# Splitting 128-column fp32 products into two 64-column products on the two halves of PSUM

## The chip, the cores and the metric

The kernel runs on one core of one Trainium2 chip. The metric is device time in microseconds for one execution of the whole program. Of the kernel before, three runs were timed: 2756.0, 2758.8 and 2760.12 us, with a median of 2758.8 us.

## The reference

The program is a two-layer decoder trunk on 256 tokens and 2048 channels, all in fp32. Layer 0 mixes tokens with a gated DeltaNet (32 value heads, 16 key heads), layer 1 with HGRN2 (16 heads); each is followed by a SwiGLU feed-forward layer. Cut to what matters here:

```python
def gated_delta_rule_chunked(q, k, v, beta, g):      # GDN, chunks of 64 tokens
    A = strict_lower(kb @ k.T * decay)
    T = triangular_solve(eye + A, eye)               # per head and chunk
    u, w = T @ (v * b), T @ (kb * exp(G))
    for chunk:
        v_new = u - w @ S
        o = q_dec @ S + (q @ k.T * decay) @ v_new
        S = S * g_last + k_dec.T @ v_new

def hgrn2_chunked(q, k, v, logf):
    for chunk:
        o = q_dec @ S + scores @ v
        S = S * f_last + k_dec.T @ v

h = h + gdn_mixer(rmsnorm(h)); h = h + swiglu(rmsnorm(h))
h = h + hgrn2_mixer(rmsnorm(h)); h = h + swiglu(rmsnorm(h))
out = rmsnorm(h)
```

## The kernel before, in words

Nearly all arithmetic is the dense projections. Their weights stream from HBM in pieces of 128 x 1024 fp32 values (512 KB, here called halves), issued by SP into the tiles `raw`, of which there are four. ACT rounds each half into `wh` (type fp32r), DVE takes the remainder into `wl`, and TensorE adds three fp32r products (high x high, high x low, low x high) into the PSUM tiles `main`. One half feeds twelve products with 512 moving columns. These are the main products.

Between them lie the batches of the recurrences, which use plain fp32 operands and write the PSUM tiles `aux`. A plain fp32 product stands in the profile as two records (two weight loads and two matmuls), a main product as one. For each of the eight groups of four GDN heads these batches follow one another:

- In `gdn_qk` (line 1039), twice a group: `k` against `k` and `q` (`aux<-kqv`, 512 and 256 moving columns), and behind them two products of the squares `sq` with a single column of ones (`aux<-ones,sq`).
- In `gdn_inverse` (line 1129): `aux<-inv,nmat` and `aux<-u,pp`, first in blocks of 32 columns and then of 64. The 64-column blocks write the lower and the upper 64 partitions of PSUM in turn.
- In `gdn_o` (line 1302): `aux<-r,u`, `aux<-w,nmat`, again `aux<-r,u` (four products of 128 stationary and 128 moving columns each), and twelve in `aux<-w,dec`.

For each of the four groups of four HGRN heads, `hgrn_scores` (line 1487) has one batch of four products with 128 stationary and 128 moving columns (`aux<-qp,kp 128*128`), then three batches with 64 stationary columns and 32 or 64 moving ones (`aux<-qp,kp 128*64`, `aux<-q,k`), whose outputs go to the two PSUM halves in turn; `hgrn_o` (line 1624) has twelve products in one batch (`aux<-v,sc`, `aux<-v,cross`).

The order of all instructions is made when the program is built. Calls are recorded (class `Recorder`), and `plan` (line 310) plays them through on one clock for each engine, with a price for every operation from `price` (line 262), then issues them in the order it found, all from line 490. For fp32 products the price depends on the number of stationary columns, whatever moves: 0.075 us up to 64 columns, at least 0.224 us above that. Each change between main and recurrence products is priced at 0.06 us. `batches` (line 289) lets a batch start only when all that its products read is ready. On the chip every engine then runs its list strictly in order.

Two paths go through DRAM. `gdn_inverse` gathers a triangular matrix by four SP loads (`wide<-n_dram`, line 1135), which stand in SP's queue among the loads of weight halves; `conv_turned` (line 1004) and `through_dram` (line 769) transpose keys and queries by DMAs from the POOL queue into `kq_blocks`, which ACT copies to `pre`.

The function below prices the products; the functions after it hold those that the change touches.

```python
m = op.args[1].shape[1]
op.cost = 0.05 if m <= 32 else 0.075 if m <= 64 else max(FP32_PRODUCT, n * 1.69e-3)
```

Of the kernel before, what the change touches and what calls it, by code (L numbers as in the profile page):

```python
# [17 lines left out]
P = 128  # L18
T = 256
# [486 lines left out]
class Trunk:  # L506
# [282 lines left out]
    def keep_x(self):  # L789

        self.resident = self.nc.pool("resident", 1, phase=True)
        for cg in range(2):
            self.x[cg] = self.tile(self.resident, [P, 2, 512], f"resident{cg}")
            self.nc.gpsimd.dma_start(self.x[cg], self.x_cols(self.x_home, cg))

    def load_x(self, cg):
        if self.resident:
            return
        self.x[cg] = self.tile(self.xpool, [P, 2, 512], "x", ordered=True)
        self.nc.gpsimd.dma_start(self.x[cg], self.x_cols(self.x_at, cg))  # L800
# [238 lines left out]
    def gdn_qk(self, hg, pre, st):  # L1039
        nc = self.nc  # L1040
        t = lambda shape, tag, **kw: self.tile(self.pool, shape, tag, **kw)
        kq = t([P, 4, T], "kqv")
        self.conv_silu(pre, [16 + 2 * hg, 2 * hg, 17 + 2 * hg, 2 * hg + 1], kq)


        g_row = t([P, 1024], "g_row")
        nc.gpsimd.dma_start(
            g_row,
            self.g_rows[4 * hg : 4 * hg + 4, :].rearrange("h t -> (h t)").unsqueeze(0).broadcast_to([P, 1024]),
        )  # L1050
        rows = g_row.rearrange("p (h c s) -> p h c s", h=4, s=CH)
        dec = t([P, 4, 384], "dec", bufs=2)
        for tt in range(2):
            part = dec[:, :, tt * T : tt * T + T - tt * P]
            for c in range(4 - 2 * tt):
                for h in range(4):
                    at = 4 * tt + c
                    nc.scalar.activation(
                        part[:, h, c * CH : (c + 1) * CH], rows[:, h, 2 * tt + c, :], AF.Relu,
                        bias=self.shift[:, 4 * hg + h, at : at + 1], scale=-1.0,  # L1060
                    )
        nc.scalar.activation(dec, dec, AF.Exp, scale=-1.0)
        for tt in range(2):
            own = dec[:, :, tt * T : tt * T + P]
            nc.gpsimd.affine_select(
                out=own, in_=own, pattern=[[0, 4], [1, P]], compare_op=ALU.is_ge, fill=0.0,
                base=0, channel_multiplier=-1,
            )


        ss, pw, rec = (t([P, 2, 4], n, bufs=2) for n in ("ssqk", "pwqk", "recqk"))
        nmat = t([P, 4, 384], "nmat", bufs=2)
        for kh in range(2):
            k = kq[:, 2 * kh, :]
            both = kq[:, 2 * kh : 2 * kh + 2, :]
            ps0, ps1 = self.aux(), self.aux()
            nc.together(ps0, ps1, nmat)
            nc.after(dec)
            nc.tensor.matmul(
                ps0, k[:, 0:P], both.rearrange("p a t -> p (a t)"), start=True, stop=True  # L1080
            )
            nc.after(dec)
            nc.tensor.matmul(
                ps1[:, 0:T].rearrange("p (a t) -> p a t", a=2), k[:, P:T], both[:, :, P:T],
                start=True, stop=True,
            )
            sq = t([P, T], "sq", bufs=2)
            nc.scalar.activation(sq, both[:, 1, :], AF.Square)
            for tt in range(2):
                nc.tensor.matmul(  # L1090
                    ps1[:, T + tt : T + tt + 1], sq[:, tt * P : (tt + 1) * P], self.ones[:, 0:1],
                    start=True, stop=True,
                )
            for tt, ps in enumerate((ps0, ps1)):
                nc.vector.scalar_tensor_tensor(
                    out=self.vjunk[:, 0:P], in0=ps[:, 0:P], scalar=1.0, in1=self.ident,
                    op0=ALU.mult, op1=ALU.mult, accum_out=ss[:, kh, 2 * tt : 2 * tt + 1],
                )
            nc.vector.tensor_copy(ss[:, kh, 1:4:2], ps1[:, T : T + 2])
            nc.vector.tensor_scalar(  # L1100
                out=ss[:, kh, :], in0=ss[:, kh, :], scalar1=1e-6, scalar2=None, op0=ALU.add
            )
            nc.gpsimd.tensor_tensor(out=pw[:, kh, :], in0=ss[:, kh, :], in1=self.expo, op=ALU.pow)
            nc.vector.reciprocal(out=rec[:, kh, :], in_=ss[:, kh, :])
            heads = slice(2 * kh, 2 * kh + 2)
            for ps, tt, w in ((ps0, 0, T), (ps1, 1, P)):
                d = dec[:, heads, tt * T : tt * T + w]
                for at, o in ((0, nmat[:, heads, tt * T : tt * T + w]), (w, d)):
                    nc.vector.scalar_tensor_tensor(
                        out=o, in0=ps[:, at : at + w].unsqueeze(1).broadcast_to([P, 2, w]),  # L1110
                        scalar=rec[:, kh, 2 * tt : 2 * tt + 1], in1=d, op0=ALU.mult, op1=ALU.mult,
                    )
        pw = pw.rearrange("p k (t c) -> p k t c", c=2)
        st["inv_k"], st["q_scale"] = pw[:, :, :, 0], pw[:, :, :, 1].rearrange("p k t -> p t k")
        st["n"], st["scores"] = nmat, dec


        n_dram = self.tile(self.dram, [32, 32, 32], "n_dram")
        u_dram = self.tile(self.dram, [32, 32, 32], "u_dram")
        for q in range(4):  # L1120
            b = slice(32 * q, 32 * q + 32)
            for tt in range(2):
                nc.gpsimd.dma_start(
                    n_dram[8 * q + 4 * tt : 8 * q + 4 * tt + 4].rearrange("a j i -> j a i"),
                    nmat[b, :, 256 * tt + 32 * q : 256 * tt + 32 * q + 32],
                )
        st["n_dram"], st["u_dram"] = n_dram, u_dram
# [174 lines left out]
    def gdn_o(self, hg, st):  # L1302
        nc = self.nc
        n, sc, u, r = st["n"], st["scores"], st["u"], st["r"]

        def heads(ps, lhs, rhs, start=True, stop=True):
            for h in range(4):
                nc.tensor.matmul(ps[:, h * P : (h + 1) * P], lhs(h), rhs(h), start=start, stop=stop)

        def evac(ps):  # L1310
            w = self.tile(self.pool, [P, 512], "w", bufs=2)
            nc.scalar.activation(w, ps, AF.Copy)
            return lambda h: w[:, h * P : (h + 1) * P]

        ps = self.aux()
        heads(ps, lambda h: u[:, h, :], lambda h: r[:, 0, h, :])
        w1 = evac(ps)
        ps = self.aux()
        heads(ps, lambda h: n[:, h, P:T], w1)
        r1 = r[:, 1, :, :].rearrange("p h d -> p (h d)")  # L1320
        nc.vector.tensor_tensor(out=r1, in0=r1, in1=ps, op=ALU.subtract)
        ps = self.aux()
        heads(ps, lambda h: u[:, 4 + h, :], lambda h: r[:, 1, h, :])
        w2 = evac(ps)
        o = [self.aux(), self.aux()]
        nc.together(*o)
        nc.after(w2(0))
        heads(o[0], lambda h: sc[:, h, 0:P], w1)
        for h in range(4):
            s = o[1][:, h * P : (h + 1) * P]  # L1330
            nc.after(w2(0))
            nc.tensor.matmul(s, sc[:, h, P:T], w1(h), start=True, stop=False)
            nc.tensor.matmul(s, sc[:, h, T:384], w2(h), start=False, stop=True)
        scale = self.tile(self.pool, [P, 8], "oscale")
        nc.vector.tensor_single_scalar(
            out=scale.rearrange("p (t k e) -> p t k e", t=2, e=2),
            in_=st["q_scale"].unsqueeze(3).broadcast_to([P, 2, 2, 2]),
            scalar=float(P) ** -0.5, op=ALU.mult,
        )
        st["ot"] = self.head_out(  # L1340
            o, st["zs"], scale, self.gdn_hn, r.rearrange("p t h d -> p (t h d)")
        )
# [144 lines left out]
    def hgrn_scores(self, g, rows, st):  # L1487
        nc = self.nc
# [27 lines left out]
        tt(qp, q[:, :, P:T], e[:, :, P:T], ALU.mult)  # L1516
        ps = self.aux()
        for h in range(4):
            nc.tensor.matmul(
                ps[:, h * P : (h + 1) * P], kp[:, h, 0:P], qp[:, h, :], start=True, stop=True  # L1520
            )
        cross = t([P, 512], "cross", bufs=2)
        nc.scalar.activation(cross, ps, AF.Copy)
        st["cross"] = cross
# [60 lines left out]
        for n in range(0, len(LEVELS), 2):  # L1585
            ps = self.aux()
# [37 lines left out]
    def hgrn_o(self, g, st):  # L1624
# [4 lines left out]
        for tok in range(2):  # L1629
            for h in range(4):  # L1630
                s = slice(h * P, (h + 1) * P)
                if tok:
                    nc.after(sc)
                    nc.tensor.matmul(o[1][:, s], cross[:, s], v[:, 0, s], start=True, stop=False)
                nc.tensor.matmul(
                    o[tok][:, s], sc[:, 2 * h + tok, :], v[:, tok, s], start=not tok, stop=True
                )
        st["ot"] = self.head_out(
            o, st["zs"], 0.5, self.hgrn_hn, v.rearrange("p t c -> p (t c)")
        )  # L1640
# [197 lines left out]
```

## Time and profile before

| | |
|---|---|
| median of three runs | 2758.8 us |
| the profiled execution's own time | 2763.12 us |
| its span | 2761.4 us |
| granted TensorE clock over the span | 0.997 |
| PE busy | 2740.1 us, 99% |
| DVE / ACT / POOL busy | 64% / 53% / 16% |
| main products on the chain that ended last | 88% of the span |
| recurrence products on that chain | 6% of the span |

How to read it: busy time of PE counts overlapped matmuls once, and a matmul's end is modelled, so it tells only that PE seldom stands idle. What a product costs is read from the starts of consecutive matmuls in the timeline. A row such as `aux<-r,u 128*128 128x128 f32 x8` gives 128 rows by 128 stationary columns, then partitions by moving columns, and the number of records (two for a product).

### The profile page before, as it was taken

The numbers are of one execution on the slowest core, as the hardware profiler recorded it, in microseconds if no ns is written. First come the engines' busy times: TensorE is split into PE (matmuls) and PEld (weight loads), VectorE is DVE, ScalarE is ACT, GpSimd is POOL, SyncE is SP. The second block draws the span as 40 slices with busy tenths as digits, with TensorE's granted clock in tenths as the row PEclk, the third lists the DMA queues.
The fourth block names the chain that finished last, engine by engine and source line by source line (L and its number), as shares of the span: only waits on it lengthen the run. The fifth ranks groups of instructions, "written<-read, shape, count | busy, mean of one in ns | idle before, by whom it ended". The sixth has DMA issues, their size and how long they took to land.

```text
span 2761.4 us, 38131 instructions
## 1 busy us (share of the span) xinstructions
PE 2740.1 (99%) x13938; PEld 2271.5 (82%) x13938; DVE 1779.8 (64%) x2637; ACT 1449.9 (53%) x2048; POOL 449.9 (16%) x711
## 2 busy tenths in 40 slices
PE   9999999999999999999999999999999999999998
PEld 8888788788887888888888888888888888888887
DVE  6887798788665555545555676787665555455554
ACT  7656575775544444334444566576454444344443
POOL 2323333233221111001111101110011110001100
PEclk9999999999999999999999999999999999999999
DMA  7887888778796666666667767665676676666664
GB/s 250 238 275 230 251 251 281 241 221 270 254 308 223 217 220 219 195 193 216 218 219 228 219 189 230 192 213 175 207 240 217 216 217 208 194 208 217 217 207 152
DMA packets 177227, 616.83 MB, mean 223 GB/s; under 512 B 25786, under 2 KB 26954, under 8 KB 176912
## 3 DMA queue, kind: packets, MB, share of 16 engines
q1 hardware_dynamic: 138912, 503.15, 56.9%
q0 software_dynamic: 37840, 110.40, 13.5%
q8 instruction: 109, 1.79, 0.3%
q10 hardware_dynamic: 288, 0.85, 0.1%
q14 instruction: 78, 0.64, 0.1%
HBM read 569.17 MB, written 45.13 MB: 222 GB/s over the span
## 4 chain that ended last, share of the span: by engine, by line
PE 94%; DMA 3%; issue 1%; DVE 1%; ACT 0%; POOL 0%; SPq 0%; POOLq 0%; ACTq 0%; DVEq 0%
PE main L490 88%; PE aux L490 6%; DMA rows<-wide 1%; DMA raw<-in_gdn_z 0%; DMA raw<-in_gdn_out 0%; DMA kq_blocks<-rows 0%; DMA kqv<-rows 0%; DMA rows<-kq_blocks 0%; ACT wh L490 0%; DVE wl L490 0%; DMA first<-in_x 0%; DVE x L490 0%; DMA x_home<-x 0%; POOL x_home L490 0%; DVE zs L490 0%
## 5 line engine op out<-in xcount | busy, mean ns | idle before, releaser
L490 DVE TENSOR_TENSOR wl<-raw,wh 128x1024 fp32r<-128x1024 f32 x945 | 1157.9, 1226 | 900.5 <-ACT wh L490 896.7
L490 ACT ACTIVATE wh<-raw 128x1024 fp32r<-128x1024 f32 x945 | 1000.6, 1060 | 1199.6 <-PE main L490 1138.0
L490 PE MATMUL main<-wl,xt_h 128*128 128x512 f32 x2656 | 1038.7, 391 | 0.0
L490 PE MATMUL main<-wh,xt_h 128*128 128x512 f32 x2656 | 1038.2, 391 | 0.0
L490 PE MATMUL main<-wh,xt_l 128*128 128x512 f32 x2656 | 1037.7, 391 | 0.0
L490 PEld LDWEIGHTS main<-wh,xt_h 128*128 128x128 f32 x2656 | 499.7, 188 | 103.4 <-ACT wh L490 0.2
L490 PEld LDWEIGHTS main<-wh,xt_l 128*128 128x128 f32 x2656 | 499.8, 188 | 103.0
L490 PEld LDWEIGHTS main<-wl,xt_h 128*128 128x128 f32 x2656 | 499.8, 188 | 102.9
L490 PE MATMUL main<-wh,hth 128*128 128x512 f32 x664 | 258.3, 389 | 0.0
L490 PE MATMUL main<-wl,hth 128*128 128x512 f32 x664 | 258.3, 389 | 0.0
L490 PE MATMUL main<-wh,htl 128*128 128x512 f32 x664 | 258.3, 389 | 0.0
L490 POOL DMA_DIRECT2D rows<-blocks x44 | 33.6, 764 | 902.0 <-DVE blocks L490 870.9
L490 PE MATMUL main<-wh,ot_h 128*128 128x512 f32 x384 | 150.6, 392 | 0.0
L490 PE MATMUL main<-wh,ot_l 128*128 128x512 f32 x384 | 150.1, 391 | 0.0
L490 PE MATMUL main<-wl,ot_h 128*128 128x512 f32 x384 | 150.0, 391 | 0.0
L490 PEld LDWEIGHTS main<-wl,hth 128*128 128x128 f32 x664 | 124.6, 188 | 26.0
L490 PEld LDWEIGHTS main<-wh,hth 128*128 128x128 f32 x664 | 124.6, 188 | 25.9
L490 PEld LDWEIGHTS main<-wh,htl 128*128 128x128 f32 x664 | 124.6, 188 | 25.8
L490 POOL DMA_DIRECT2D h<-rows x176 | 96.1, 553 | 189.9 <-issue 81.6
L490 PEld LDWEIGHTS main<-wh,ot_l 128*128 128x128 f32 x384 | 72.1, 188 | 14.8
L490 PEld LDWEIGHTS main<-wh,ot_h 128*128 128x128 f32 x384 | 72.1, 188 | 14.7
L490 PEld LDWEIGHTS main<-wl,ot_h 128*128 128x128 f32 x384 | 72.1, 188 | 14.5
(244 smaller groups left out, 2040.3 us busy)
## 6 DMA issues: line engine op xcount, KB each, us to landing
raw<-in_ffn_gu SPq DMA_DIRECT2D x352, 512.0 KB, 4.5
raw<-in_ffn_d SPq DMA_DIRECT2D x176, 512.0 KB, 4.4
raw<-in_hgrn_in SPq DMA_DIRECT2D x128, 512.0 KB, 4.2
raw<-in_gdn_kq SPq DMA_DIRECT2D x64, 512.0 KB, 5.2
raw<-in_gdn_v SPq DMA_DIRECT2D x64, 512.0 KB, 4.9
raw<-in_gdn_z SPq DMA_DIRECT2D x64, 512.0 KB, 5.0
raw<-in_gdn_out SPq DMA_DIRECT2D x64, 512.0 KB, 6.2
raw<-in_hgrn_out SPq DMA_DIRECT2D x32, 512.0 KB, 3.7
```

The lines of the kernel that those rows point to most:

```text
L490: getattr(getattr(tc.nc, op.eng), op.method)(*args, **kw)
```

## The change

A new method `product` replaces the plain call in five places: it cuts the stationary operand into columns 0 to 63 and 64 to 127, and issues a product for each with all moving columns, writing PSUM partitions 0 to 63 and 64 to 127. The five places are the products with `sq`, the three kinds of `heads` calls and the last twelve products of `gdn_o`, the cross products of `hgrn_scores` and the products of `hgrn_o`. The products of `kqv` (512 and 256 moving columns) stay as they are.

```diff
+    def product(self, out, lhs, rhs, start=True, stop=True):
+        for side in range(2):
+            s = slice(side * 64, side * 64 + 64)
+            self.nc.tensor.matmul(out[s], lhs[:, s], rhs, start=start, stop=stop)
...
             for tt in range(2):
-                nc.tensor.matmul(
-                    ps1[:, T + tt : T + tt + 1], sq[:, tt * P : (tt + 1) * P], self.ones[:, 0:1],
-                    start=True, stop=True,
-                )
+                self.product(ps1[:, T + tt : T + tt + 1], sq[:, tt * P : (tt + 1) * P], self.ones[:, 0:1])
...
         def heads(ps, lhs, rhs, start=True, stop=True):
             for h in range(4):
-                nc.tensor.matmul(ps[:, h * P : (h + 1) * P], lhs(h), rhs(h), start=start, stop=stop)
+                self.product(ps[:, h * P : (h + 1) * P], lhs(h), rhs(h), start, stop)
...
-            nc.tensor.matmul(s, sc[:, h, P:T], w1(h), start=True, stop=False)
-            nc.tensor.matmul(s, sc[:, h, T:384], w2(h), start=False, stop=True)
+            self.product(s, sc[:, h, P:T], w1(h), True, False)
+            self.product(s, sc[:, h, T:384], w2(h), False, True)
...
-            nc.tensor.matmul(
-                ps[:, h * P : (h + 1) * P], kp[:, h, 0:P], qp[:, h, :], start=True, stop=True
-            )
+            self.product(ps[:, h * P : (h + 1) * P], kp[:, h, 0:P], qp[:, h, :])
...
-                    nc.tensor.matmul(o[1][:, s], cross[:, s], v[:, 0, s], start=True, stop=False)
-                nc.tensor.matmul(
-                    o[tok][:, s], sc[:, 2 * h + tok, :], v[:, tok, s], start=not tok, stop=True
-                )
+                    self.product(o[1][:, s], cross[:, s], v[:, 0, s], True, False)
+                self.product(o[tok][:, s], sc[:, 2 * h + tok, :], v[:, tok, s], not tok, True)
```

Since `price` gives a 64-column product 0.075 us, the planner prices the two halves at 0.15 us together where it had 0.224 us, and its order differs from the first changed batches on. TensorE, second group of GDN heads, around the first batch of `gdn_o` (`r` and `u` feed `heads`; a shape here is stationary columns by moving columns, and a count is of products). Before:

```order
L490 MATMUL main_2487<-wh_2566,xt_h_15_71 128x512
L490 MATMUL aux_2722<-r_353,u_2117 128x128 x4
L490 MATMUL main_2487<-wl_2582,xt_h_15_71 128x512
L490 MATMUL main_2487<-wh_2566,xt_l_19_75 128x512
L490 MATMUL main_2487<-wh_2615,xt_h_15_71 128x512
...
L490 MATMUL main_2487<-wl_2628,xt_h_15_71 128x512
L490 MATMUL aux_2738<-w_2728,nmat_345 128x128 x4
```

With the change:

```order
L490 MATMUL main_2774<-wh_2630,xt_l_16_72 128x512
L490 MATMUL aux_2786<-r_353,u_2222 64x128 x8
L490 MATMUL main_2774<-wh_2630,xt_h_12_68 128x512
L490 MATMUL main_2774<-wl_2681,xt_h_12_68 128x512
L490 MATMUL main_2774<-wh_2630,xt_l_16_72 128x512
...
L490 MATMUL main_2774<-wh_2678,xt_h_12_68 128x512
L490 MATMUL aux_2811<-w_2799,nmat_345 64x128 x8
```

Each batch is one visit of eight halved products between main products, as it was one visit of four whole ones; seven main products lie between the two batches before and with the change.

ACT, the sixth group of keys and queries: the two copies out of the main tile (`acc<-main`) that begin the transpose, and the copies into `pre` that end it, with the casts `wh` of weight halves between. Before (eight casts lie between):

```order
L490 ACTIVATE acc_4887<-main_4647,rstd_61 128x512
...
L490 ACTIVATE pp_5078<-aux_5057 32x8x32 x2
L490 ACTIVATE wh_5094<-raw_5006 128x1024
L490 ACTIVATE r_5115<-main_4861,rstd_61 128x512
L490 ACTIVATE u_4418<-aux_5097 32x8x32 x2
L490 ACTIVATE r_5115<-main_4861,rstd_61 128x512
L490 ACTIVATE pre_4259<-kq_blocks_4909 128x4x128
L490 ACTIVATE wh_5145<-raw_5020 128x1024
L490 ACTIVATE pp_5161<-aux_5143 64x4x64 x2
```

With the change (thirteen casts lie between the copies out of the main tile and this place):

```order
L490 ACTIVATE wh_5286<-raw_5216 128x1024
L490 ACTIVATE pp_5309<-aux_5282 32x8x32 x2
L490 ACTIVATE pre_4418<-kq_blocks_5099 128x4x128 x2
L490 ACTIVATE u_4581<-aux_5326 32x8x32 x2
L490 ACTIVATE wh_5359<-raw_5240 128x1024
L490 ACTIVATE acc_5369<-pre_4418,conv_325 128x256 x2
```

In all seven transposes of keys and queries the casts between number 7, 7, 8, 13, 10, 8 and 6 before, and 10, 11, 18, 14, 10, 13 and 12 with the change.

DVE, the third group's inverse: the transposes into `inv`, which the batch `inv,nmat` reads, and the remainders `wl` ahead of them. In SP's queue `raw_3319` is the first half behind the loads `wide_3297`, as `raw_3393` is the first behind `wide_3373` with the change. Before:

```order
L490 TENSOR_TENSOR wl_3376<-raw_3287,wh_3366 128x1024
L490 TENSOR_TENSOR wl_3395<-raw_3319,wh_3386 128x1024
L490 STREAM_TRANSPOSE inv_2675<-u_2786 32x8x32 x2
L490 SCALAR_TENSOR_TENSOR acc_3404<-pre_1857,conv_325,acc_3404 128x256
L490 STREAM_TRANSPOSE inv_2675<-u_2786 32x8x32
```

With the change:

```order
L490 TENSOR_TENSOR wl_3457<-raw_3357,wh_3444 128x1024
L490 TENSOR_TENSOR wl_3475<-raw_3393,wh_3465 128x1024
L490 TENSOR_TENSOR wl_3499<-raw_3418,wh_3487 128x1024
L490 STREAM_TRANSPOSE inv_2740<-u_2847 32x8x32 x2
L490 SCALAR_TENSOR_TENSOR acc_3507<-pre_1940,conv_325,acc_3507 128x256
L490 STREAM_TRANSPOSE inv_2740<-u_2847 32x8x32
```

The transposes stood behind the remainder of the first half behind `wide`; now they stand behind that of the second.

## The prediction

> **What bounds the kernel now.** I read the page first, busy times and the chain of waits:
>
> ```profile
> PE 2740.1 (99%) x13938; PEld 2271.5 (82%) x13938; DVE 1779.8 (64%) x2637; ACT 1449.9 (53%) x2048; POOL 449.9 (16%) x711
> PE 94%; DMA 3%; issue 1%; DVE 1%; ACT 0%; POOL 0%; SPq 0%; POOLq 0%; ACTq 0%; DVEq 0%
> ```
>
> TensorE is almost never without work, and 94% of the chain is TensorE. So whatever the change adds to TensorE's list or takes from it arrives at the end nearly whole; other engines count only where TensorE stands still. The chain in order of time gives the pace of the main products:
>
> ```profile
> 837.06 714.71 PE main L490 x3153
> ```
>
> 714.71 / 3153 = 0.227 us from start to start. Next the groups of instructions by form, for how many records the change touches (two records make a product):
>
> ```profile
> L490 PE MATMUL aux<-w,dec 128*128 128x128 f32 x192 | 22.7, 275 | 0.0
> L490 PE MATMUL aux<-r,u 128*128 128x128 f32 x128 | 16.9, 275 | 0.0
> L490 PE MATMUL aux<-v,sc 128*128 128x128 f32 x64 | 10.5, 276 | 0.0
> L490 PE MATMUL aux<-w,nmat 128*128 128x128 f32 x64 | 8.4, 274 | 0.0
> L490 PE MATMUL aux<-ones,sq 128*128 128x1 f32 x64 | 8.0, 229 | 0.0
> L490 PE MATMUL aux<-v,cross 128*128 128x128 f32 x32 | 6.2, 275 | 0.0
> L490 PE MATMUL aux<-qp,kp 128*128 128x128 f32 x32 | 4.2, 274 | 0.0
> ```
>
> 192 + 128 + 64 + 64 + 32 + 32 = 512 records are 256 products with 128 moving columns; 64 records are 32 products with one.
>
> **What a batch costs now.** For a batch I take the time from the start of the last main product ahead of it to the start of the second main product behind it, less two main paces (0.453 us). Timeline of PE, eight records, then 24:
>
> ```profile
> 255.86 0.39 PE L490 MATMUL main<-wh,xt_h 128*128 128x512 f32 x1
> 256.08 1.05 PE L490 MATMUL aux<-r,u 128*128 128x128 f32 x8
> 256.89 0.48 PE L490 MATMUL main<-wl,xt_h 128*128 128x512 f32 x1
> 257.21 0.40 PE L490 MATMUL main<-wh,xt_l 128*128 128x512 f32 x1
> ```
> ```profile
> 264.02 0.39 PE L490 MATMUL main<-wh,xt_h 128*128 128x512 f32 x1
> 264.24 2.84 PE L490 MATMUL aux<-w,dec 128*128 128x128 f32 x24
> 266.84 0.48 PE L490 MATMUL main<-wl,xt_h 128*128 128x512 f32 x1
> 267.15 0.40 PE L490 MATMUL main<-wh,xt_l 128*128 128x512 f32 x1
> ```
>
> 257.21 - 255.86 - 0.453 = 0.90 us, and 267.15 - 264.02 - 0.453 = 2.68 us. Sixteen records more cost 1.78 us: 0.111 us a record, 0.223 us a product, and nothing fixed (0.90 - 8 x 0.111 = 0.01). Going from main products to a whole-width batch and back is free.
>
> **What a batch of 64-column products costs.** The kernel has such batches already, with outputs on the two sides in turn, though with 64 and 32 moving columns only:
>
> ```profile
> 249.87 0.39 PE L490 MATMUL main<-wh,xt_l 128*128 128x512 f32 x1
> 250.19 0.68 PE L490 MATMUL aux<-inv,nmat 64*64 64x64 f32 x16
> 250.80 0.50 PE L490 MATMUL main<-wh,xt_h 128*128 128x512 f32 x1
> 251.14 0.39 PE L490 MATMUL main<-wl,xt_h 128*128 128x512 f32 x1
> ```
> ```profile
> 1638.19 0.39 PE L490 MATMUL main<-wl,xt_h 128*128 128x512 f32 x1
> 1638.51 2.06 PE L490 MATMUL aux<-qp,kp 128*64 128x32 f32 x64
> 1640.50 0.50 PE L490 MATMUL main<-wh,xt_l 128*128 128x512 f32 x1
> 1640.84 0.39 PE L490 MATMUL main<-wh,xt_h 128*128 128x512 f32 x1
> ```
>
> Now it is 1.27 - 0.453 = 0.82 us for 16 records and 2.65 - 0.453 = 2.20 us for 64. 48 records more cost 1.38 us, 0.029 us a record, or 0.058 us for one on each side. What is left over is fixed: 0.82 - 16 x 0.029 = **0.36 us a visit**. One sees where it lies: the first record comes 0.32 us after the main product ahead (0.22 in the whole-width batches), and the first main product behind takes 0.34 us to the next.
>
> **The records themselves.** Batches with `sq` show how fast plain fp32 columns stream:
>
> ```profile
> 67.85 0.42 PE L490 MATMUL main<-wh,xt_h 128*128 128x512 f32 x1
> 68.11 1.45 PE L490 MATMUL aux<-kqv 128*128 128x512 f32 x4
> 69.39 0.50 PE L490 MATMUL aux<-ones,sq 128*128 128x1 f32 x4
> 69.76 0.48 PE L490 MATMUL main<-wl,xt_h 128*128 128x512 f32 x1
> 70.08 0.39 PE L490 MATMUL main<-wh,xt_l 128*128 128x512 f32 x1
> ```
>
> The four `kqv` records move 2 x 512 + 2 x 256 = 1536 columns in 69.39 - 68.11 = 1.28 us: 0.83 ns a column, 0.053 us for 64, 0.107 us for 128. With 64 moving columns a pair of records, one a side, takes 0.058 us, hardly more than one stream of 64: the sides do run beside each other. With 128 moving columns each side streams for 0.107 us, so a pair should take 0.11 us. A halved product is two pairs, 0.22 us, what the whole one costs now. Bounds: a pair cannot be cheaper than the 0.058 us seen with 32 columns (the weight load's pace), and if the sides don't overlap at all it is 2 x 0.111. I take 0.111, the stream's, as the pace of `kqv` and the pair with 64 columns both lie on it. So the records change nothing, and each visit adds 0.36 us.
>
> [...]
>
> **Visits.** In the changed order the halved products with 128 moving columns stand in 4 x 8 visits in the gated DeltaNet, and in 4 + 4 in HGRN2, of which two are one (a cross batch within an output batch): 39 x 0.36 = **+14.0 us**. The `sq` products sit behind `kqv`, which stays whole, so each of the 16 batches turns once more. Now: 70.08 - 67.85 - 0.453 - 1.28 = 0.50 us. After: 8 x 0.029 + 0.36 = 0.59 us. 16 x 0.09 = **+1.5 us**.
>
> **The waits.** TensorE does stand still in the gated DeltaNet, in few places. Two wide ones in the timeline of PE, then of ACT, and the stages around them (window, length, busy time of PE, PEld, DVE, ACT and POOL, then the granted clock, 0.87 and 0.93 of full speed):
>
> ```profile
> 329.39 0.39 PE L490 MATMUL main<-wh,xt_h 128*128 128x512 f32 x1
> 332.90 1.43 PE L490 MATMUL aux<-inv,nmat 32*32 32x32 f32 x32 [3.13 <-DVE inv L490]
> 503.68 0.39 PE L490 MATMUL main<-wh,xt_h 128*128 128x512 f32 x1
> 505.99 1.37 PE L490 MATMUL aux<-u,pp 64*64 64x64 f32 x16 [1.92 <-ACT pp L490]
> ```
> ```profile
> 330.10 1.06 ACT L490 ACTIVATE wh<-raw 128x1024 fp32r<-128x1024 f32 x1 [5.45 <-DMA raw<-in_gdn_z]
> 503.96 0.63 ACT L490 ACTIVATE pre<-kq_blocks 128x512 f32<-128x512 f32 x1 [3.16 <-DMA kq_blocks<-rows]
> ```
> ```profile
> 320.00:360.00 40.00, 36.78 (x237) 29.50 (x236) 26.45 (x61) 22.63 (x36) 9.43 (x17) 0.87 0.79 230
> 495.00:520.00 25.00, 23.00 (x183) 18.39 (x183) 18.18 (x53) 16.29 (x27) 2.30 (x4) 0.93 0.78 231
> ```
>
> The first costs 3.51 - 0.32 = 3.2 us, and the clock granted after it 0.13 x 40 = 5.2 us; the second 2.31 - 0.32 = 2.0 us and 0.07 x 25 = 1.7 us. The second starts as ACT waits for transposed keys ahead of `pp`. In the changed order thirteen casts instead of eight lie between the start of that transpose and its use; a half feeds twelve main products (2.7 us), so some 13 us more cover a wait of 3.16 us: I let it go, **-3.7 us**. The first starts at a weight half that is queued on SP right behind the four `wide` loads. DVE's transposes for `inv` still stand behind such halves (the second instead of the first), so I leave it. Which other halves come late in the new order can't be read off: one such wait more is +8.4 us, this one gone -8.4 us. TensorE being slower than planned, not faster, gives loads a little more time.
>
> What hides the rest: ACT's and DVE's copies out of the halved batches are as long as before, and as many main products lie between a batch and the next that needs it.
>
> **Sum.** The profiled execution took 2763.1 us, and 14.0 + 1.5 - 3.7 = +11.8 us makes 2774.9. It lay 4.3 us above the median of the runs, so for the median 2758.8 + 11.8 = 2770.6, said as **2771 us**.
>
> **The rivals.**
>
> 1. Another late half (or the transposed keys late elsewhere): turns +15.5 us, both old waits kept in kind and up to one added: +15.5 to +24, 2774 to 2783. For it speaks that two of the eight groups wait like this now; against it the longer leads.
> 2. The late half at 330 us goes too: +15.5 - 3.7 - 8.4 = +3.4, 2762 us, no change that can be told. Its place in the queue speaks against it.
> 3. Faster: weight loads, not streams, set the pace of a pair, 0.058 us with 128 columns too. Then four products are 8 x 0.058 + 0.36 = 0.82 us against 0.90 and twelve 24 x 0.058 + 0.36 = 1.75 against 2.68: 27 x -0.08 + 12 x -0.93 + 1.5 = -11.8 us, with the wait that goes 2743 us. It decides as soon as a pair takes under 0.08 us. `kqv`'s 0.83 ns a column speaks against it.
> 4. The sides don't overlap with 128 columns: 512 pairs at 0.222 instead of 0.111 us, +57 us more, 2828 us. The pair with 64 columns speaks against it.
> 5. The load of a side's weights does not overlap its stream: a pair takes 0.058 + 0.107 = 0.165 us, 512 x 0.054 = +28 us more, 2798 us. The same row speaks against it. [...]
> 6. The change does not do what it says: the visits take no turn, since here all 128 rows and both sides are filled by the same operand. Then +0 - 3.7, 2755 us. The 64-record batch above has 128 rows and both sides too, and pays.
>
> **How the numbers follow.** A measurement of this kernel can tell about 0.2% (5.5 us) from no change. Forecast 0.56, rival 1 0.22, rival 2 0.10, rival 3 0.04, rivals 4 and 5 0.02 each, rival 6 0.04. Low end: rival 2's 2762 less 2 for the spread of runs; high end: rival 1's 2783 and 2 more. Rivals 3 to 6 and a few tails stay out. Slower: forecast, 1, 4, 5 and a little of 2: 0.83. Same: most of 2, and 6: 0.12. Faster: 3 and a little of 6: 0.05.
>
> **What would show it.** In the timeline after, the batch `aux<-r,u 128*64 128x128 x16` measured in the same way takes 1.25 us (0.82 if rival 3 holds, 2.1 if rival 4), `aux<-w,dec` with 48 records 3.0 us, starting 0.32 us after the main product ahead. The wait of ACT for `kq_blocks` ahead of `pp` is gone, that of DVE's `inv` is there. I am wrong if visits cost nothing, if a pair is far from 0.11 us, or if waits with a halved clock move by more than 10 us.

## The result and the profile after

The changed kernel takes 2786.8 us (median, 2785.6 to 2793.3) against 2758.3 us before: the ratio is 1.0109, 95% interval 1.0091 to 1.0126. The forecast was 2771 us in a range of 2760 to 2785: slower, as forecast, but by 28 us instead of 12, and 2 us outside the range.

The page of the changed kernel, busy times and the chain of waits:

```profile
span 2784.5 us, 39291 instructions
PE 2750.8 (99%) x14514; PEld 2259.9 (81%) x14514; DVE 1775.9 (64%) x2637; ACT 1447.8 (52%) x2047; POOL 450.3 (16%) x711
PE 76%; DMA 3%; DVE 1%; issue 1%; ACT 1%; POOL 0%; POOLq 0%; DVEq 0%; ACTq 0%
```

The span grew by 23.1 us and PE's busy time by only 10.7: more than half of the loss, 12.4 us, is time in which TensorE stands still. (The profiled execution of before took 4.9 us more than the median, so these two spans lie closer than the medians.) First the halved batches, in the timeline of PE of the changed kernel, four products (16 records) and twelve (48):

```profile
268.81 0.39 PE L490 MATMUL main<-wl,xt_h 128*128 128x512 f32 x1
269.13 1.09 PE L490 MATMUL aux<-r,u 128*64 128x128 f32 x16
270.15 0.50 PE L490 MATMUL main<-wh,xt_l 128*128 128x512 f32 x1
270.49 0.40 PE L490 MATMUL main<-wh,xt_h 128*128 128x512 f32 x1
...
271.65 0.39 PE L490 MATMUL main<-wh,xt_l 128*128 128x512 f32 x1
271.96 2.89 PE L490 MATMUL aux<-w,dec 128*64 128x128 f32 x48
274.79 0.50 PE L490 MATMUL main<-wh,xt_h 128*128 128x512 f32 x1
275.12 0.39 PE L490 MATMUL main<-wl,xt_h 128*128 128x512 f32 x1
```

In the prediction's measure (last main start ahead to second main start behind, less 0.453 us) the first takes 270.49 - 268.81 - 0.453 = 1.23 us, where a whole one took 0.90, and the second 275.12 - 271.65 - 0.453 = 3.02 us, where it took 2.68. Both lie on the forecast of 1.25 and 3.0. Over all visits (24 batches of four and 8 of twelve in the gated DeltaNet, HGRN2's, and 16 with `sq` at 0.08 more) this makes some +14.5 us.

Most of what else is lost stands in one place, the end of the gated DeltaNet. Timeline of PE, then of ACT, pieces of the chain of waits in order of time, and the stage with its granted clock (0.80), followed by the two parts of it in which the clock is at half (0.51 and 0.50):

```profile
795.59 0.39 PE L490 MATMUL main<-wh,ot_l 128*128 128x512 f32 x1
807.77 0.80 PE L490 MATMUL main<-wh,ot_h 128*128 128x512 f32 x1 [11.80 <-ACT ot_h L490]
808.36 0.63 PE L490 MATMUL main<-wl,ot_h 128*128 128x512 f32 x1
809.48 0.80 PE L490 MATMUL main<-wh,ot_l 128*128 128x512 f32 x1 [0.48 <-DVE ot_l L490]
```
```profile
806.57 1.15 ACT L490 ACTIVATE ot_h<-zs,gdn_hn 128x1024 fp32r<-128x1024 f32 x1 [9.51 <-DMA zs<-rows]
```
```profile
773.43 2.82 PE aux L490 x48
782.57 2.35 POOL ocol L490
785.79 4.25 issue
790.05 6.95 DMA rows<-r
798.95 7.52 DMA zs<-rows
806.57 1.16 ACT ot_h L490
```
```profile
795.00:830.00 35.00, 22.72 (x90) 17.87 (x89) 14.62 (x16) 11.37 (x16) 8.04 (x13) 0.80 0.66 202
799.00:807.00 8.00, 0.00 (x0) 0.00 (x0) 0.00 (x0) 0.43 (x1) 1.23 (x2) 0.51 0.90 213
807.00:812.00 5.00, 3.74 (x8) 2.56 (x9) 1.67 (x4) 0.72 (x1) 0.00 (x0) 0.50 0.00 0
```

The last group's twelve products end at 773.43 + 2.82 = 776.25 us. Their normalisation, the way through DRAM and the cast to `ot_h` are done at 807.72, 31.5 us later. TensorE has main products only until 795.8 us, then it needs `ot_h` for the last out projection: it waits 11.8 us. The clock of 0.80 makes 0.20 x 35 = 7.0 us less clock, but the spell of half clock begins at 799.2 us, inside the wait, and lasts 13.65 us (the clock's records in the trace). Some 8.5 us of it pass while TensorE has nothing to do and cost nothing; in the 5.1 us behind the wait TensorE is busy for 4.6 us, which costs some 2.3 us. (The expectations below still count 7 us.) The kernel before has the same path in ACT's timeline and in its chain of waits:

```profile
777.07 1.15 ACT L490 ACTIVATE ot_h<-zs,gdn_hn 128x1024 fp32r<-128x1024 f32 x1 [1.43 <-PE main L490]
```
```profile
744.19 2.68 PE aux L490 x24
746.87 24.96 PE main L490 x110
```

There the batch ended at 746.87 and `ot_h` at 778.22: 31.4 us too, though 2.6 us of this are not the path's. The last load of `zs` landed at 774.48 us, but the cast started only at 777.07, when TensorE released it; the path itself took some 29 us. And 41.2 us of main products stood between that batch and the first use, and nothing waited; in the changed order it is 19.5 us (main products between, counted in the lists, at 0.227 us). Of the two waits that the prediction knew, the late half near 330 us no longer holds up `inv`: 0.93 us for `r` is left in that stage, with the clock whole. The wait for `pp` is gone, with 1.42 us for `inv` in its stage:

```profile
338.91 0.50 PE L490 MATMUL main<-wh,xt_h 128*128 128x512 f32 x1 [0.93 <-ACT r L490]
519.79 0.68 PE L490 MATMUL aux<-inv,nmat 64*64 64x64 f32 x16 [1.42 <-DVE inv L490]
```
```profile
320.00:360.00 40.00, 39.07 (x275) 30.70 (x274) 32.95 (x71) 26.46 (x42) 12.19 (x21) 1.00 0.87 280
```

A new one, of 2.91 us for `inv`, stands at 674.6 us (shown in the last section): DVE's transposes stood in its list behind an operation that waited for a DMA.

```profile
673.50 1.23 DVE L490 TENSOR_TENSOR before<-before,taps 128x1024 f32<-128x1024 f32 x1 [4.58 <-DMA before<-v_rows]
```

So of 23.1 us: 12.4 us are TensorE standing still longer (span less busy time: 33.7 against 21.3 us), and the waits for `ot_h` and `ot_l` are 11.8 + 0.5 = 12.3 of them; all other waits together are as long as before, at other places. The 10.7 us of busy time are the turns' +14.5 and the half clock, which costs 2.3 us here and cost 6.6 in the execution before (the prediction took 5.2 + 1.7 from two windows): -4.3; 0.5 us are left over. The whole loss by `ot_h` is thus 12.3 + 2.3 = +14.6 us.

### The profile page after: what moved, and what is told of

Same layout as the page of the kernel before. It is cut to its first block, busy times and chain, and to the rows that moved or that the text cites. A ratio compares the mean times of both kernels' runs of the same rounds, so it can differ in the third digit from the quotient of the medians.

```text
span 2784.5 us, 39291 instructions
## 1 busy us (share of the span) xinstructions
PE 2750.8 (99%) x14514; PEld 2259.9 (81%) x14514; DVE 1775.9 (64%) x2637; ACT 1447.8 (52%) x2047; POOL 450.3 (16%) x711
## 4 chain that ended last, share of the span: by engine, by line
PE 76%; DMA 3%; DVE 1%; issue 1%; ACT 1%; POOL 0%; POOLq 0%; DVEq 0%; ACTq 0%
PE main L490 72%; PE aux L490 4%; DMA before<-v_rows 0%; DMA rows<-wide 0%; DMA raw<-in_hgrn_in 0%; DMA kqv<-rows 0%; DMA v_rows<-r 0%; ACT wh L490 0%; DMA zs<-rows 0%; DMA rows_in<-rows 0%; DMA rows<-r 0%; DVE wl L490 0%; ACT e L490 0%; DVE x L490 0%; DVE r L490 0%
## 5 line engine op out<-in xcount | busy, mean ns | idle before, releaser
L490 PE MATMUL main<-wh,ot_h 128*128 128x512 f32 x384 | 151.6, 395 | 11.8 <-ACT ot_h L490 11.8
```

The lines of the kernel that those rows point to most:

```text
L490: getattr(getattr(tc.nc, op.eng), op.method)(*args, **kw)
```

## The experiments

The theory after this: the form (halves) costs its turns, and the order (from the planner's price of 0.15 us for a halved product) costs the wait for `ot_h`. The rival: the halves cause all of it on the chip. The first two kernels separate form and order exactly: all five engines' lists are the same but for the form of the products.

**Halves in the order of before.** Planned as whole products, cut when issued:

```diff
-        for side in range(2): ... self.nc.tensor.matmul(out[s], lhs[:, s], rhs, ...)
+        self.nc.tensor.matmul(out, lhs, rhs, start=start, stop=stop)
+        self.nc.ops[-1].cut = True
...
+                if op.cut:
+                    for s in (slice(0, 64), slice(64, P)):
+                        tc.nc.tensor.matmul(args[0][s], args[1][:, s], args[2], **kw)
+                    continue
```

> The halved products stand exactly where the whole ones stood: the planner plays whole products at 0.224 us, and each is issued as its two halves, so all five engines' lists are those of before except for the halves. Theory (the planner's price of 0.15 us moves the gated DeltaNet's batches late, and the wait of 11.8 us for ot_h with the half clock behind it comes from that order): only the turns are left, 24 visits of four products at +0.33, 8 of twelve at +0.34, HGRN2's 8 at +0.33, 16 behind kqv at +0.08, together some +14 us: 2772 us, between 2764 and 2778 as old waits shift; no wait for ot_h. Rival (the halves themselves cause the whole loss, by waits around each visit): 2787 us.

Measured: 2773.3 us, ratio 1.0044 (1.0027 to 1.0060). Timeline of PE and two stages of this kernel:

```profile
257.73 0.39 PE L495 MATMUL main<-wh,xt_h 128*128 128x512 f32 x1
258.05 1.09 PE L493 MATMUL aux<-r,u 128*64 128x128 f32 x16
259.07 0.50 PE L495 MATMUL main<-wl,xt_h 128*128 128x512 f32 x1
259.41 0.40 PE L495 MATMUL main<-wh,xt_l 128*128 128x512 f32 x1
```
```profile
320.00:360.00 40.00, 39.00 (x299) 30.46 (x299) 31.76 (x68) 26.44 (x42) 10.54 (x18) 1.00 0.90 268
495.00:520.00 25.00, 23.19 (x202) 17.67 (x202) 18.16 (x52) 16.79 (x27) 2.15 (x4) 1.00 0.81 236
```

The batch costs 259.41 - 257.73 - 0.453 = 1.23 us again, no wait for `ot_h` exists, and the time is as the theory said. The clock stays whole in both stages where it fell before; that a slower TensorE waits less for the same late loads would explain it, but is only argued.

**Whole products in the changed order.** Planned as halves, each pair issued as one:

```diff
             self.nc.tensor.matmul(out[s], lhs[:, s], rhs, start=start, stop=stop)
+            self.nc.ops[-1].whole = (out, lhs, rhs) if side else ()
...
+                if op.whole == ():
+                    continue
-                args = [self.actual(a) for a in op.args]
+                args = [self.actual(a) for a in op.whole or op.args]
```

> The order of the changed kernel with whole products: planned as halves, each pair issued as one whole product, so all lists are those of the changed kernel except for the halves. Theory (the order makes the wait): the wait for ot_h near 796 us stays at some 10 to 13 us with about 7 us of half clock behind it; 2786.8 less 14 us of turns = 2773 us, between 2766 and 2778. Rival (the halves themselves cause the loss): 2758 us and no wait for ot_h. A second rival, that a slower TensorE caused the wait by reaching the last batches late: the wait shrinks to under 4 us and the time is about 2762.

Measured: 2773.7 us, ratio 1.0047 (1.0031 to 1.0063). Timeline of PE and the stage with its clock:

```profile
782.97 0.39 PE L493 MATMUL main<-wh,ot_l 128*128 128x512 f32 x1
793.55 0.79 PE L493 MATMUL main<-wh,ot_h 128*128 128x512 f32 x1 [10.19 <-ACT ot_h L493]
```
```profile
780.00:815.00 35.00, 24.32 (x94) 19.07 (x93) 14.34 (x16) 11.06 (x13) 7.71 (x13) 0.80 0.66 212
```

The wait is there without a single halved product. So the order makes it, and both rivals fall. The two ratios multiply to 1.0091, the lower end of the interval of the changed kernel's 1.0109 (1.0091 to 1.0126): within the noise, form and order add up.

**One side, then the other.** Each batch issues all its lower halves, then all its upper ones:

```diff
-                    for s in (slice(0, 64), slice(64, P)):
-                        tc.nc.tensor.matmul(args[0][s], args[1][:, s], args[2], **kw)
+                    for s in (slice(0, 64), slice(64, P)):
+                        for o in run:
+                            out, lhs, rhs = [self.actual(a) for a in o.args]
+                            tc.nc.tensor.matmul(out[s], lhs[:, s], rhs, **o.kw)
```

> As the halves in the old order, but a batch issues all its lower halves first and then all its upper halves, so the sides are not in turn. If two records overlap only when they stand on different sides one behind the other, a record costs the stream's 0.107 to 0.111 us: a batch of 16 records 16 x 0.11 + 0.36 = 2.1 us instead of 1.22, one of 48 records 5.6 us instead of 3.02, in all some 55 to 60 us over the halves in the old order: about 2830 us. If the array overlaps them anyway, the batch stays at 1.22 us and the time at 2772.

Measured, one run: 2818.7 us. Timeline of PE:

```profile
262.68 0.39 PE L512 MATMUL main<-wh,xt_h 128*128 128x512 f32 x1
262.99 1.58 PE L510 MATMUL aux<-r,u 128*64 128x128 f32 x16
264.51 0.50 PE L512 MATMUL main<-wl,xt_h 128*128 128x512 f32 x1
264.84 0.39 PE L512 MATMUL main<-wh,xt_l 128*128 128x512 f32 x1
```

264.84 - 262.68 - 0.453 = 1.71 us, between the two expectations, 0.5 us over the sides in turn; batches of 48 records take 5.2 us instead of 3.0, much nearer to the first. With the sides in turn a pair of halves takes 0.112 us ((3.02 - 1.23) / 16); one side after the other, 32 records more cost 5.2 - 1.71 = 3.5 us, 0.109 us for each. So taking the sides in turn is what lets most of the halves run beside each other; without it the same work costs some 45 us more in this one run.

**Cut, whole, cut.** In batches of twelve, the middle four products stay whole:

```diff
-                if op.cut:
+                if op.cut and where[op] // 4 % 2 == 0:      # place of the product in its batch
```

> The halves in the old order, but in the batches of twelve products the middle four stay whole: cut, whole, cut. If a fixed price is paid for each excursion to the 64-column form, whatever the length, such a batch turns twice: 24 records of 0.111 us' worth and 2 x 0.30 to 0.34, 3.3 us instead of 2.97. If the price belongs to a batch (to its beginning and end between main products), it stays at 2.97; if it belongs to halved products, each paying a share, it falls to some 2.87. In time of the program 12 x 0.33 = 4 us over the halves in the old order at most, about 2776 us.

Measured, one run: 2776.4 us. Timeline of PE:

```profile
267.45 0.39 PE L500 MATMUL main<-wh,xt_h 128*128 128x512 f32 x1
267.77 1.09 PE L498 MATMUL aux<-w,dec 128*64 128x128 f32 x16
268.80 1.16 PE L500 MATMUL aux<-w,dec 128*128 128x128 f32 x8
269.88 1.09 PE L498 MATMUL aux<-w,dec 128*64 128x128 f32 x16
270.91 0.50 PE L500 MATMUL main<-wl,xt_h 128*128 128x512 f32 x1
271.25 0.40 PE L500 MATMUL main<-wh,xt_l 128*128 128x512 f32 x1
```

271.25 - 267.45 - 0.453 = 3.35 us, against 2.97 us for the batch with one excursion in the same order (the halves in the order of before). The second excursion costs 0.38 us more, with whole products between, where one between main products costs some 0.33: here the price is paid for each excursion into the 64-column form.

**True prices.** The changed kernel, with the planner told what the traces show:

```diff
-                op.cost = 0.05 if m <= 32 else 0.075 if m <= 64 else ...
+                op.cost = 0.05 if m <= 32 else max(0.058, n * 0.87e-3) if m <= 64 else ...
...
-                op.cost += TURN * (op.main != streaming)
-                streaming = op.main
+                kind = "main" if op.main else "cut" if ... op.args[1].shape[1] <= 64 else "whole"
+                op.cost += CUT_TURN * ("cut" in (kind, streaming) and kind != streaming)   # 0.18
+                streaming = kind
```

> The changed kernel with prices as the profiles show them: a 64-column fp32 product 0.058 us or 0.87 ns a moving column, whichever is more, and 0.18 us for each change into or out of such products (0 between main and whole ones, which had 0.06). The last batch of twelve then stands 35.6 us of main products ahead of the last group's first use in the out projection, against 19.5 in the changed kernel and 41.2 before. Theory (too low a price made the late order): no wait of more than 2 us for ot_h, and the turns' 14 us are left: 2772 us, between 2762 and 2780. Rival (any new order of this planner brings some 12 us of waits): about 2785.

Measured: 2773.2 us, ratio 1.0040 (1.0025 to 1.0055). Its waits on PE hold only this of the out projection:

```profile
PE main L491 <- DVE ot_l L491: 0.6, 1, 0.6
```

As expected: the wait for `ot_h` goes with the wrong prices, the turns' cost stays. The edit changes two prices, that of a halved product and that of a turn, so it does not say which of them brings the lead back.

**Whole products with better prices.** Since order alone is worth 12 us, three orders of the kernel before were tried: the turn's price (with 0.06 instead of 0.075 us for a 64-column product); a later landing of halves behind `wide`; and both.

```diff
+                kind = ...                                   # as above, 0.18 us a change
...
+                if "wide" in tags:
+                    wide_at = at
+                elif "raw" in tags and at < wide_at + 6.0:
+                    op.lag = 10.0
```

> The kernel before, whole products, but planned with 0.18 us for each change into or out of 64-column products (instead of 0.06 for any change from or to main products) and 0.06 instead of 0.075 us for such a product. TensorE's work is the same; only the order differs. Theory (the order's waits are worth some 10 us, and true prices make fewer): the half clock after 330 us goes, 2747 to 2758 us. Rival (any new order has as many waits): 2755 to 2772 us.

> The kernel before, whole products and its own prices, but the planner takes 10 us instead of 4.8 for a weight half that is issued within 6 us behind the wide loads, near what the trace of before shows (8 to 14 us from issue to use). Theory (the wait at 330 us is a half late behind wide, worth 8.4 us with its half clock): 2748 to 2755 us, no wait of over 1.5 us for inv. Rival (the wait moves to another place): 2756 to 2770 us.

> Both of the planner's corrections together, whole products. The last batch of twelve stands only 27 us of main products ahead of the last group's use in the out projection (41 before, 19.5 in the changed kernel). From the changed kernel's trace that path takes some 31 us, so a wait of about 4 us for ot_h is expected, and the clock's half speed if it passes some 3 us: 2758 to 2768 us. If leads have nothing to do with that wait: 2748.

Measured: 2762.9 us, ratio 1.0016 (1.0004 to 1.0029); 2758.7 us, 0.9998 (0.9986 to 1.0011); 2759.9 us, 1.0002 (0.9992 to 1.0013). Each removed some waits and got others: the first two expectations, of several us gained, failed. The third has the short lead of 27 us and shows the wait that this calls for, in its timeline of PE:

```profile
780.55 0.50 PE L498 MATMUL main<-wh,ot_h 128*128 128x512 f32 x1 [2.19 <-ACT ot_h L498]
782.35 0.50 PE L498 MATMUL main<-wh,ot_l 128*128 128x512 f32 x1 [1.07 <-DVE ot_l L498]
...
783.43 0.63 PE L498 MATMUL main<-wh,ot_h 128*128 128x512 f32 x1
783.86 0.63 PE L498 MATMUL main<-wl,ot_h 128*128 128x512 f32 x1
784.29 0.63 PE L498 MATMUL main<-wh,ot_l 128*128 128x512 f32 x1
```

The 3 us of wait that its expectation names for half clock lie between the waits of 2.91 us (clock whole) and 3.13 us (half) and are an estimate; no run shows them as a limit: behind these waits of 2.19 and 1.07 us the main products come 0.43 us apart, as in the half clock of the kernel before (0.43 us from 339.56 to 339.99 us).

The last try adds slack ahead of each recurrence batch (0.9 us for 0.5, and 8.5 us for the landing):

> Whole products, planned with all that the traces showed: 0.18 us for each change into or out of 64-column products, 8.5 us for weight halves issued within 6 us behind the wide loads, and 0.9 instead of 0.5 us of slack ahead of a recurrence batch. The last batch of twelve stands 40.6 us of main products ahead of the last group's use in the out projection. Theory (the path to ot_h takes 29 to 35 us, and what the lead falls short of it is waited for): no wait for ot_h. If the other waits shrink with the larger slack, the time is 2746 to 2754 us; if they only move, 2756 to 2764.

Measured: 2754.6 us against 2759.3, ratio 0.9982 (0.9973 to 0.9992), the fastest kernel here, just above the range expected for shrinking waits. In its waits on PE there is none for `ot_h`; the largest entry is this:

```profile
PE aux L498 <- DVE inv L498: 4.0, 4, 2.1
```

Its span is 9.8 us shorter than that of before, and the 6.6 us that half clock cost there are most of it: in this execution the granted clock is 1.00 from 40 to 840 us, and 0.999 over the span against 0.997.

Lead and wait side by side (main products between the last batch of twelve and the first use of `ot_h` from it, against the waits for `ot_h` and `ot_l`): 41.2 us none; 40.6 none; 35.6 0.6 us; 27.0 3.3 us; 19.5 10.7 us with whole products and 12.3 with halves. The path from that batch's end to the end of the cast, read from the kept traces, is not fixed: 35.2 us with true prices (lead 35.6), 29.1 with both corrections (lead 27.0), 29.7 and 31.5 in the changed order with whole and halved products (lead 19.5). What the lead lacks is each time the wait for `ot_h`: none, 2.2, 10.2 and 11.8 us. With true prices it was just long enough.

## Why the prediction was wrong, and where it was right

**Turns and records: right.** A visit was priced at 0.36 us with nothing gained on the records; it costs 0.33 (1.23 against 0.90, 3.02 against 2.68). The sum for the form, +15.5 us, stands against some +14.5 from the batches. In the order of before the halves made the program only 12 us slower, since in its trace TensorE stands still 2.2 us less than before and no half clock is left (granted clock 0.999 over the span against 0.997, where half clock cost 6.6 us). That a pair of records with 128 moving columns takes the stream's 0.11 us was an extrapolation from 64 columns; it held ((3.02 - 1.23) / 16 = 0.112 us a pair), so rivals 3, 4, 5 and 6 fell. Rival 5's pair of 0.165 us would, as an estimate, have put a batch of four at some 1.7 us (8 x 0.165 + 0.36); 1.23 was measured with the sides in turn.

**"As many main products lie between a batch and the next that needs it": the step that failed.** It was looked up for the batches within a group, and there it is so. It was not looked up for the last consumer of a group, the out projection. Counted there, the lists show 41.2 and 19.5 us, and the trace of before shows `ot_h` 31.4 us behind that batch, of which some 29 us were the path. Both numbers were to be had, and they give 9.5 to 11.9 us of waiting where the prediction put nothing; 11.8 came for `ot_h`, 0.5 for `ot_l` and some 2.3 us of half clock, together 14.6. That it came out at the upper end is partly chance: the changed kernel's own path took 31.5 us, other orders 29 to 35.

**The two old waits: half right.** The one for transposed keys went, as said, though 1.42 us for `inv` came in its stage. The late half at 330 us was kept at its full price of 8.4 us, as its place in the queues had not changed; it went. Its time of standing still came back elsewhere (2.91 us at 674.6 us), its 5.2 us of half clock did not. That was luck: it made the miss smaller.

**Rival 1** named another wait of unknown place, up to 2783 us, and is the nearest of the cases. Its reason, another late transfer, fits the small wait of 2.91 us, behind the DMA into `before`. It was not the reason of the large one: there the use came early against the batch.

**Why the order moved.** The planner takes the halves for 0.15 us instead of 0.224. In the gated DeltaNet that is 192 + 32 products x 0.074 = 16.6 us of TensorE time that it believes saved, and the last batch stands 41.2 - 19.5 = 21.7 us of main products later. Whole products planned at that price show the same wait, and their planning differs from that of before only in the two halves and their price: that the price brought the late order is shown. Halves at true prices fit it, but there the turn's price changed too. That the 16.6 us are the whole of the 21.7 is only argued; the planner's choices jump, as the lead of 27 us with dearer turns shows.

## What to carry to other kernels

Cutting a stationary operand in two gained nothing here, where a pair of halves with 128 moving columns took 0.112 us and a record of the whole product 0.111, and each excursion from full-width products into the 64-column form cost some 0.33 us; at that price it can pay only for batches that the halves shorten by more. When an order is made from prices, a wrong price for one operation can cost far from that operation: check, for every producer on a long path (here 29 to 35 us through DRAM), how much independent work the new order leaves until its last consumer, not only until the next step. Half clock that passed while TensorE waited anyway cost nothing here (8.5 of 13.65 us): multiply the clock that is missing only with the time behind the wait. Separate form and order in two kernels that share all lists; their effects added up here to the lower end of the measured whole.

## What the runs showed of the hardware that was not expected

With all lower halves ahead of all upper ones, 16 records took 1.71 us where strictly one after another 16 x 0.109 + 0.34 = 2.08 us was expected, and 48 took 5.2 instead of 5.6: both are some 0.4 us short, the same for both lengths, which is the time of some four records (4 x 0.109 = 0.44 us). Where the batch gains it is open.

The clock did not follow the length of a wait alone. In the kernel before it fell to half with waits of 3.13 and of 1.92 us (granted clock 0.50 from 332.53 to 342.77 us and from 506.61 to 510.02 us); in the kernel before it stayed whole through 2.87 us at 833.1 us (1.00 from 828 to 836 us), and in the changed kernel through 2.91 us (timeline of PE, and its stage):

```profile
674.21 0.39 PE L490 MATMUL main<-wh,ot_h 128*128 128x512 f32 x1
677.51 0.68 PE L490 MATMUL aux<-inv,nmat 64*64 64x64 f32 x16 [2.91 <-DVE inv L490]
```
```profile
660.00:700.00 40.00, 37.09 (x312) 29.04 (x312) 28.27 (x53) 20.74 (x41) 11.99 (x19) 1.00 0.97 296
```

The spells of half clock up to the last matmul last 10.24 and 3.41 us in the kernel before, and 13.65 us in the changed kernel with its wait of 11.8 us (the clock's records in the two traces). A wait of 1.92 us had one and a wait of 2.91 us had none, so no length of a wait from which the clock falls can be read from these traces. By these runs a price for half the clock belongs to a wait only with a chance.
